# Both MLPs of a decoder step with their first product by Strassen's quadrants, the hidden units through DRAM, and the state-space matrices made beside layer 0's second product

## The chip, the cores and the metric

The kernel runs on one core of a Trainium2 chip. Its time is the device time of one execution in microseconds. Three runs of the kernel before took 2729.11, 2738.31 and 2733.10 us, the median 2733.1. One further execution was profiled: it took 2730.87 us, and 2729.1 us lie between its first and its last instruction (the span). All times of instructions below are from that execution.

## The reference

One inference step through four sublayers: layer 0 has an attention and convolution mixer and an MLP, layer 1 a state-space mixer (S5) and an MLP. A prompt of 1024 tokens and 8 x 4 sample tokens go through the same weights. All is float32. The MLP, with its norms before and after and its residual, is what the change rewrites:

```python
D_MODEL = 1024; D_FF = 4 * D_MODEL
def sq_relu_mlp(xn, w_up, w_down):
    return jnp.square(jax.nn.relu(xn @ w_up)) @ w_down
...
hp = hp + rms_norm(sq_relu_mlp(rms_norm(hp, g_ffn_pre[l]), w_ffn_up[l], w_ffn_down[l]), g_ffn_post[l])
hs = hs + rms_norm(sq_relu_mlp(rms_norm(hs, g_ffn_pre[l]), w_ffn_up[l], w_ffn_down[l]), g_ffn_post[l])
```

The state-space mixer runs a diagonal complex recurrence with 64 groups of 64 states. Its matrices depend on the weights alone (a, b, c and the time step):

```python
dt = jnp.exp(log_dt)[:, None]
mag = jnp.exp(a_re * dt); ang = a_im * dt
ab_re, ab_im = mag * jnp.cos(ang), mag * jnp.sin(ang)
...
bu = einsum('blgc,gpc->blgp', ug, bb)           # real and imaginary part
h = associative_scan over the tokens            # h_t = ab * h_(t-1) + bu_t
y = einsum('blgp,gcp->blgc', h_re, c_re) - einsum('blgp,gcp->blgc', h_im, c_im)
```

## The kernel before

The activations are kept transposed: 8 tiles of 128 features by 1056 tokens, worked on in three chunks of 352 tokens. Every large product is done in split precision: each operand is a high part (`zh`, `whi`, `hh`) and a low part (`zl`, `wlo`, `hl`), and one product of 128 by 128 by 352 is three matmuls (`mm3`, L190): high by high, low by high, high by low. `block` (L197) strings them over the k tiles of one output tile. The high part is a cast on ScalarE (L186, L216), the low part a subtraction on VectorE (L187, L217). SBUF holds 48 slabs of 128 x 1056 float32, handed out and taken back in program order, and some half tiles of 352.

`ffn` (L481) runs one MLP as a list of units. An up unit makes 128 hidden features: 3 chunks of 24 matmuls, each evicted by VectorE (relu times the norm's factor, L502), squared on ScalarE (L503) and split into `hh` and `hl`, which stay in SBUF. After a group of hidden units (2 in layer 0, 4 in layer 1) come down units, which multiply the group by a piece of the second weight matrix and add the result to the eight output tiles `y` (L537). Weights are loaded two units ahead (`wprep`, L179). The last four down units lie inside `posts` (L386), chunk by chunk, each followed by `post` (L303): norm, residual, and the split of the next layer's operands.

What runs beside is a generator: `bg_add` and `pump` (L100, L104) advance it by so many microseconds of its own estimates per unit of the MLP, times a rate. `params5` (L1599) makes the state-space matrices: factors on VectorE, ten doublings of a rotation, then on GpSimd sixteen tables of 128 x 1024, each built from the rotations by complex products (`cmul`, L1590 and on) and written to DRAM (`tabs<-tc`), then b and c, which are turned on TensorE (`cT`, L1766) and combined on GpSimd into eight blocks (`bd`, `ws`, `tmat`). In before it is started ahead of layer 0's MLP with rate 0.7 (`tile_step`, L2103).

A scheduler sets the order of the compute instructions of each engine from its own estimates and the dependencies. Each engine then runs its list strictly in that order. All DMAs of the program go through one queue, SP's (`dma`, L92), and they keep the order in which the program issues them: a transfer whose data isn't ready holds back every transfer behind it.

## Time and profile before

| | |
|---|---|
| runs | 2729.11, 2738.31, 2733.10 us (median 2733.1) |
| profiled execution | 2730.87 us, span 2729.1 us |
| granted TensorE clock, mean | 0.968 |
| TensorE busy | 2562.5 us, 94% of the span |
| VectorE, ScalarE, GpSimd busy | 1573.2, 984.3 and 739.7 us |
| moved by DMA | 276.72 MB, mean 101 GB/s |

The page's busy time is an average over the whole program. By stretch, layer 0's MLP lies from about 760 to 1440 us of the span and layer 1's from about 1990 to the end. A matmul's record is longer than the distance to the next one, since they are pipelined: the price of one in a full stream is the stretch divided by the number of matmuls, or the distance of two starts. On SP a row is one transfer's issue; a transfer that waits appears late, with the reason in the waits.

### The profile page before, as it was taken

Reading aid. Unit: us, or ns where it says so; the run is one execution under the profiler, and the core shown is the slowest. Engines: PE = TensorE matmul, PEld = TensorE weight load, DVE = VectorE, ACT = ScalarE, POOL = GpSimd, SP = SyncE. Lnnn points to the kernel's source line nnn. Section 1 sums busy time; section 2 is a strip of 40 time slices with the busy share of each in tenths; the row PEclk is TensorE's granted clock in tenths of the full one; section 3 lists DMA queues with packets and bytes.
Section 4 is the critical chain, followed back from the end, with each engine's and each line's share of the span. In section 5 each row is a group of like instructions: output and inputs, shape, how many; then the busy total and the mean of one; then the engine's idle time right before and its main releaser. Section 6 shows DMA issues by size and latency. Waiting matters only on the chain. (4 is left out here: it accounts for less than half of the span.)

```text
span 2729.1 us, 41453 instructions
## 1 busy us (share of the span) xinstructions
PE 2562.5 (94%) x15979; PEld 2431.6 (89%) x15979; DVE 1573.2 (58%) x2802; ACT 984.3 (36%) x2032; POOL 739.7 (27%) x1090
## 2 busy tenths in 40 slices
PE   8999889789899999999998888799899999999998
PEld 7999756559799999999998877699799999999997
DVE  6776666753967555655545998941833334333335
ACT  6133355744441212123224566633533112211223
POOL 0110001111607874344303588611600000000004
PEclk9999989999899999999999999899899999999999
DMA  6353689563132223122312533113121111111121
GB/s 188 94 171 113 203 289 325 169 206 94 44 97 60 88 86 92 52 89 83 104 55 66 170 116 131 40 30 118 59 89 55 47 47 47 42 44 40 55 95 64
DMA packets 244828, 276.72 MB, mean 101 GB/s; under 512 B 26452, under 2 KB 179810, under 8 KB 244623
## 3 DMA queue, kind: packets, MB, share of 16 engines
q1 hardware_dynamic: 244299, 273.84, 31.6%
q8 instruction: 126, 2.06, 0.3%
q14 instruction: 71, 0.58, 0.1%
q10 hardware_dynamic: 332, 0.23, 0.0%
HBM read 218.03 MB, written 56.42 MB: 101 GB/s over the span
## 5 line engine op out<-in xcount | busy, mean ns | idle before, releaser
L193 PE MATMUL mm<-hh,whi 128*128 128x352 f32 x1536 | 500.9, 326 | 0.0
L195 PE MATMUL mm<-hh,wlo 128*128 128x352 f32 x1536 | 496.9, 323 | 0.0
L194 PE MATMUL mm<-hl,whi 128*128 128x352 f32 x1536 | 496.7, 323 | 0.0
L193 PE MATMUL mm<-zh,whi 128*128 128x352 f32 x1344 | 448.1, 334 | 0.2 <-ACT zh L216 0.2
L194 PE MATMUL mm<-zl,whi 128*128 128x352 f32 x1344 | 440.5, 328 | 3.9 <-DVE zl L217 3.9
L195 PE MATMUL mm<-zh,wlo 128*128 128x352 f32 x1344 | 438.2, 326 | 0.0
L537 DVE TENSOR_TENSOR y<-y,mm 128x352 f32<-128x352 f32 x456 | 229.9, 518 | 236.6 <-PE mm L195 234.8
L503 ACT ACTIVATE t<-t 128x352 f32<-128x352 f32 x192 | 95.3, 498 | 738.3 <-DVE t L502 738.3
L187 DVE TENSOR_TENSOR wlo<-wraw,whi 128x1024 fp32r<-128x1024 f32 x180 | 229.0, 1275 | 229.6 <-ACT whi L186 225.4
L291 POOL TENSOR_TENSOR ssq<-ssq,sq 128x352 f32<-128x352 f32 x72 | 72.8, 1011 | 955.5 <-issue 672.7
L193 PE MATMUL mm<-gh,whi 128*128 128x352 f32 x960 | 314.5, 328 | 0.0
L194 PE MATMUL mm<-gl,whi 128*128 128x352 f32 x960 | 311.7, 325 | 0.0
L195 PE MATMUL mm<-gh,wlo 128*128 128x352 f32 x960 | 311.5, 324 | 0.0
L193 PEld LDWEIGHTS mm<-hh,whi 128*128 128x128 f32 x1536 | 289.8, 189 | 0.6 <-issue 0.2
L194 PEld LDWEIGHTS mm<-hl,whi 128*128 128x128 f32 x1536 | 289.9, 189 | 0.5 <-issue 0.2
L195 PEld LDWEIGHTS mm<-hh,wlo 128*128 128x128 f32 x1536 | 289.6, 189 | 0.0
L186 ACT CAST whi<-wraw 128x1024 fp32r<-128x1024 f32 x180 | 187.3, 1044 | 245.9 <-DMA wraw<-in_w_ffn_up 77.9
L194 PEld LDWEIGHTS mm<-zl,whi 128*128 128x128 f32 x1344 | 258.0, 192 | 8.1 <-DVE zl L217 4.7
L193 PEld LDWEIGHTS mm<-zh,whi 128*128 128x128 f32 x1344 | 257.3, 192 | 5.9 <-issue 3.3
L195 PEld LDWEIGHTS mm<-zh,wlo 128*128 128x128 f32 x1344 | 257.4, 192 | 0.1
L502 DVE SCALAR_TENSOR_TENSOR t<-mm,r 128x352 f32<-128x352 f32 x192 | 99.9, 524 | 222.3 <-PE mm L195 220.8
L194 PEld LDWEIGHTS mm<-gl,whi 128*128 128x128 f32 x960 | 182.4, 190 | 1.0 <-issue 0.5
(485 smaller groups left out, 4564.9 us busy)
## 6 DMA issues: line engine op xcount, KB each, us to landing
pg<-in_cache_k SPq DMA_DIRECT2D x128, 256.0 KB
pg<-in_cache_v SPq DMA_DIRECT2D x128, 256.0 KB
wraw<-in_w_ffn_up SPq DMA_DIRECT2D x64, 512.0 KB
wraw<-in_w_ffn_down SPq DMA_DIRECT2D x64, 512.0 KB
hres<-res SPq DMA_DIRECT2D x24, 528.0 KB
res<-y SPq DMA_DIRECT2D x24, 528.0 KB
wraw<-in_w_in_even SPq DMA_DIRECT2D x20, 512.0 KB
tabs<-tc SPq DMA_DIRECT2D x16, 512.0 KB
```

The lines of the kernel that those rows point to most:

```text
L186: nc.scalar.copy(hi[:, :n], raw[:, :n])
L187: (eng or nc.vector).tensor_sub(lo[:, :n], raw[:, :n], hi[:, :n])
L193: nc.tensor.matmul(out, wh, xh, start=first, stop=False)
L194: nc.tensor.matmul(out, wh, xl, start=False, stop=False)
L195: nc.tensor.matmul(out, wl, xh, start=False, stop=last)
L291: (nc.vector if k in YV else nc.gpsimd).tensor_add(s, s, q)
L502: nc.vector.scalar_tensor_tensor(t1, pt, 0.0, r[:, chunk(c)], op0=ALU.max, op1=ALU.mult)
L503: nc.scalar.activation(t1, t1, AF.Square)
L537: nc.vector.tensor_add(yc, yc, pt)
```

## The change

The first product of each MLP is restated. The first four units (512 hidden features) are done as before. For the other 28, two units at a time, weights and activations are cut in quadrants (two halves of the 1024 features; two halves of the 256 hidden features; two halves of 528 tokens), and seven products of the quadrants' sums take the place of eight. Each product has 4 k tiles and 528 tokens in two pieces of 264. `sums` makes the sums of the activations as a background generator, started where the previous layer's `post` ends; `quads` makes and splits those of the weights, pair by pair, from slabs whose load is issued at the start of the pair before. The seven results are combined on the way out of PSUM in two slabs `hu` and `hv`, which get relu, factor and square over all 1056 tokens and are stored to DRAM. All 32 hidden units are loaded from DRAM again (`hr`) and split for the second product, now in eight groups of four, each step of which is 6 tiles of 12 matmuls of 352 columns. The state-space matrices are no longer started ahead of layer 0's MLP but between its two products (`beside`), with rate 1.4.

```diff
--- before
+++ after
 CH = 352
 NCH = T // CH
+T2 = T // 2
 DFF = 4096
...
             for k in range(KT):
                 self.dma(nxt[2][k], y[k])
+            if nxt[5]:
+                self.T = [[None] * 4 for _ in range(4)]
+                self.bg_add(self.sums(list(y), g2, l2, self.T), TR)
...
+    def sums(self, y, gk, l, T_):
+        nc = self.nc
+        a, b = slice(0, T2), slice(T2, T)
+        for k in range(4):
+            z1, z2 = y[k], y[k + 4]
+            y[k] = y[k + 4] = None
+            for z, k_ in ((z1, k), (z2, k + 4)):
+                nc.scalar.activation(z, z, AF.Copy, scale=self.g(gk, l, k_))
+                yield 1.1
+            nc.vector.tensor_sub(z2[:, b], z2[:, b], z1[:, b])
+            nc.vector.tensor_sub(z1[:, b], z1[:, b], z1[:, a])
+            yield 1.2
+            T_[0][k] = self.S("t1", F32R)
+            self.split(T_[0][k][:, a], T_[0][k][:, b], z1[:, b])
+            nc.vector.tensor_add(z1[:, a], z2[:, b], z1[:, a])
+            yield 1.2
+            nc.vector.tensor_sub(z2[:, a], z2[:, a], z1[:, a])
+            T_[1][k] = self.S("t2", F32R)
+            self.split(T_[1][k][:, a], T_[1][k][:, b], z1[:, a])
+            yield 1.2
+            T_[3][k] = self.S("t4", F32R)
+            self.split(T_[3][k][:, a], T_[3][k][:, b], z2[:, a])
+            T_[2][k] = z2
+            z1 = None
+            yield 1.2
+    def quads(self, R):
+        nc = self.nc
+        (a11, a21), (a12, a22) = ([r[:, :1024].rearrange("p (k j m) -> p j k m", k=4, j=2)[:, j] for j in range(2)] for r in R)
+        def part(x):
+            o = self.S("op", F32R)
+            v = [o[:, 512 * i:512 * i + 512].rearrange("p (k m) -> p k m", k=4) for i in range(2)]
+            self.split(v[0], v[1], x)
+            return v
+        yield part(a11)
+        s1 = self.S("s1")[:, :512].rearrange("p (k m) -> p k m", k=4)
+        nc.vector.tensor_add(s1, a21, a22)
+        nc.vector.tensor_sub(a21, a11, a21)
+        nc.vector.tensor_sub(a11, s1, a11)
+        yield part(a11)
+        yield part(a12)
+        nc.vector.tensor_sub(a12, a12, a11)
+        yield part(a21)
+        yield part(s1)
+        s1 = None
+        yield part(a12)
+        yield part(a22)
 
...
+    def ffn_q(self, l, X, r, res, nxt, early=None, beside=None):
+        nc = self.nc
+        w, self.pre = self.pre, {}
+        hd = self.dram.tile([32, P, T], F32, name=self.nm("hid"))
+        up_w = self.a["w_ffn_up"][l]
+        raws = {}
+        slot = [None, 3]
+        def raw(u):
+            if u < 32:
+                raws[u] = [self.S("wq") for _ in range(2)]
+                for i in range(2):
+                    self.dma(raws[u][i][:, :1024].rearrange("p (k m) -> p k m", k=4),
+                             up_w[512 * i:512 * i + 512, u * P:(u + 2) * P].rearrange("(k p) m -> p k m", p=P))
+        def up(u, c):
+            pt = self.block(w[u], slice(0, P), X, c)
+            t1 = self.H("t")
+            nc.vector.scalar_tensor_tensor(t1, pt, 0.0, r[:, chunk(c)], op0=ALU.max, op1=ALU.mult)
+            if slot[1] == 3:
+                slot[:] = self.S("hp"), 0
+            h = slot[0][:, chunk(slot[1])]
+            slot[1] += 1
+            nc.scalar.activation(h, t1, AF.Square)
+            self.dma(hd[u][:, chunk(c)], h)
+            self.pump(3.7)
+        for u in range(NB):
+            if u not in w:
+                w[u] = self.ffn_prep(l, ("u", u))
+        ops = []
+        for c in range(NCH):
+            self.chunk_ready(c)
+            if c == NCH - 1:
+                raw(NB)
+                steps = self.quads(raws[NB])
+            for u in range(NB):
+                up(u, c)
+                if c == NCH - 1:
+                    del w[u]
+                    if u:
+                        ops.append(next(steps))
+        slot[0] = None
+        self.drain()
+        B = T2
+        for k in range(4):
+            z = self.T[2][k][:, B:]
+            self.split(X[k][0][:, B:], X[k][1][:, B:], z)
+            self.T[2][k] = z = None
+        both = lambda t: [(z[:, :B], z[:, B:]) for z in t]
+        lo, hi = slice(0, B), slice(B, T)
+        rhs = [[(h[:, lo], l_[:, lo]) for h, l_ in X[:4]], both(self.T[1]), [(h[:, lo], l_[:, lo]) for h, l_ in X[4:]],
+               [(h[:, hi], l_[:, hi]) for h, l_ in X[:4]], both(self.T[0]), [(h[:, hi], l_[:, hi]) for h, l_ in X[4:]],
+               both(self.T[3])]
+        self.T = None
+        hid, wd = {}, {}
+        seq = [("d", 4 * f, 4, j) for f in range(8) for j in range(4)]
+        def prep(i):
+            if i < len(seq) and i not in wd:
+                wd[i] = self.ffn_prep(l, seq[i])
+        def hload(u):
+            if u < 32 and u not in hid:
+                z = self.S("hr")
+                self.dma(z, hd[u])
+                hid[u] = self.S("hh", F32R), self.S("hl", F32R)
+                self.split(*hid[u], z)
+        def ahead():
+            prep(0)
+            yield
+            for u in range(4):
+                if u == 2:
+                    prep(1)
+                hload(u)
+                yield
+        first, more = True, None
+        for u in range(NB, 32, 2):
+            hu, hv = self.S("hu"), self.S("hv")
+            nxt_ops = []
+            if u == 30:
+                more = ahead()
+            else:
+                raw(u + 2)
+            nsteps = None
+            for p in range(7):
+                while len(ops) <= p:
+                    ops.append(next(steps))
+                wh, wl = ops[p]
+                for x in range(2):
+                    xs = slice(264 * x, 264 * x + 264)
+                    pt = self.PS("mq")[:, :264]
+                    for k in range(4):
+                        xh, xl = rhs[p][k]
+                        self.mm3(pt, (wh[:, k], wl[:, k]), (xh[:, xs], xl[:, xs]), k == 0, k == 3)
+                    c0, c1 = slice(264 * x, 264 * x + 264), slice(B + 264 * x, B + 264 * x + 264)
+                    if p == 0:
+                        nc.scalar.copy(hu[:, c0], pt)
+                    elif p == 1:
+                        nc.vector.tensor_add(hu[:, c1], hu[:, c0], pt)
+                    elif p == 2:
+                        nc.vector.tensor_add(hu[:, c0], hu[:, c0], pt)
+                    elif p == 3:
+                        nc.vector.tensor_add(hv[:, c0], hu[:, c1], pt)
+                    elif p == 4:
+                        nc.vector.tensor_add(hu[:, c1], hu[:, c1], pt)
+                        nc.vector.tensor_add(hv[:, c1], hv[:, c0], pt)
+                    elif p == 5:
+                        nc.vector.tensor_add(hu[:, c1], hu[:, c1], pt)
+                    else:
+                        nc.vector.tensor_add(hv[:, c0], hv[:, c0], pt)
+                wh = wl = None
+                ops[p] = None
+                if p == 5:
+                    nc.vector.scalar_tensor_tensor(hu, hu, 0.0, r, op0=ALU.max, op1=ALU.mult)
+                    nc.scalar.activation(hu, hu, AF.Square)
+                    self.dma(hd[u], hu)
+                if more is not None:
+                    next(more, None)
+                elif p >= 0:
+                    if nsteps is None:
+                        nsteps = self.quads(raws[u + 2])
+                        raws.pop(u, None)
+                    nxt_ops.append(next(nsteps))
+            nc.vector.scalar_tensor_tensor(hv, hv, 0.0, r, op0=ALU.max, op1=ALU.mult)
+            nc.scalar.activation(hv, hv, AF.Square)
+            self.dma(hd[u + 1], hv)
+            ops, steps = nxt_ops, nsteps
+        X.clear()
+        rhs = xh = xl = hu = hv = nsteps = nxt_ops = pt = ops = steps = more = None
+        raws.clear()
+        for u in range(4):
+            hload(u)
+        if beside is not None:
+            beside()
+        y = [None] * KT
+        last = len(seq) - 4
+        for i, (_, f, g, j) in enumerate(seq[:last]):
+            prep(i + 2)
+            hload(f + 4 + j)
+            hs = [hid[f + i_] for i_ in range(4)]
+            for m in range(2):
+                k = 2 * j + m
+                if f == 0:
+                    y[k] = self.S("y")
+                for c in range(NCH):
+                    pt = self.block(wd[i], slice(m * P, (m + 1) * P), hs, c)
+                    yc = y[k][:, chunk(c)]
+                    if f == 0:
+                        nc.scalar.copy(yc, pt)
+                    else:
+                        nc.vector.tensor_add(yc, yc, pt)
+                    self.pump(1.84)
+            del wd[i]
+            if j == 3:
+                for i_ in range(4):
+                    del hid[f + i_]
+        for j in range(4):
+            prep(last + j)
+        self.drain()
+        hs = [hid[28 + i_] for i_ in range(4)]
...
     with s.psum():
         s.consts()
         X, r, res = s.mixer0()[:3]
-        s.bg_add(s.params5(), RP)
         nxt = s.new(X, "g_mix_pre", 1)
-        s.ffn(0, X, r, res, nxt, 2, s.mixer1_early)
+        s.ffn_q(0, X, r, res, nxt, s.mixer1_early, lambda: s.bg_add(s.params5(), RP))
         X, r, res = s.mixer1(*nxt[:3])[:3]
-        s.ffn(1, X, r, res, None, 4)
-
-
-RP = 0.7
+        s.ffn_q(1, X, r, res, None)
+RP = 1.4
```

(`new` gets a flag that asks for the sums; both callers ahead of an MLP set it.)

The scheduler's order changes with it. First, SP's queue in layer 0 near the end of the sixteen tables. `tabs` are the tables, `wraw` a weight load, `hr` a hidden unit, `b` and `cn` the state-space inputs. Before:

```order
L94 DMA wraw_1598_11206<-in_w_ffn_up 128x8x128
L94 DMA wraw_1613_11326<-in_w_ffn_up 128x8x128
L94 DMA tabs_7769<-tc_1597_11197 128x1024
L94 DMA wraw_1629_11456<-in_w_ffn_down 128x2x512
L94 DMA tabs_7769<-tc_1618_11349 128x1024
L94 DMA b_1638_11525<-in_ssm_b_re 64x32x16 x2
L94 DMA b_1638_11525<-in_ssm_b_im 64x32x16 x2
L94 DMA wraw_1643_11562<-in_w_ffn_down 128x2x512
L94 DMA wraw_1654_11666<-in_w_ffn_up 128x8x128
```

After, in the second product:

```order
L96 DMA wraw_1837_13511<-in_w_ffn_down 128x4x256
L96 DMA hr_1840_13517<-hid_1208_7736 128x1056
L96 DMA tabs_11610<-tc_1836_13496 128x1024
L96 DMA wraw_1850_13647<-in_w_ffn_down 128x4x256
L96 DMA hr_1853_13653<-hid_1208_7736 128x1056
L96 DMA tabs_11610<-tc_1846_13578 128x1024
L96 DMA tabs_11610<-tc_1857_13674 128x1024
L96 DMA b_1862_13758<-in_ssm_b_re 64x32x16 x2
L96 DMA b_1862_13758<-in_ssm_b_im 64x32x16 x2
L96 DMA wraw_1866_13779<-in_w_ffn_down 128x4x256
L96 DMA hr_1869_13785<-hid_1208_7736 128x1056
L96 DMA cn_1878_13855<-in_ssm_c_re 128x8x64 x2
```

Between two tables there were one or two weight loads; now two tables often stand with none between them, and a hidden unit goes with each weight load. From the first to the sixteenth table the new queue holds nine weight loads (before, nineteen).

Second, VectorE between the first four units on the last chunk and what follows them in layer 0. Before (`t<-mm` is an eviction, `hl` a low half):

```order
L502 SCALAR_TENSOR_TENSOR t_1273_8248<-mm_1272_8223,r_1123_7176 128x352
L217 TENSOR_TENSOR hl_1271_8222<-t_1273_8248,hh_1270_8221 128x352
L1629 COPY hs_1212_7771<-hT_1274_8253 64x256 x2
L1641 MEMSET nat_1282_8335 64x128
L502 SCALAR_TENSOR_TENSOR t_1276_8283<-mm_1275_8258,r_1123_7176 128x352
L217 TENSOR_TENSOR hl_1271_8222<-t_1276_8283,hh_1270_8221 128x352
L502 SCALAR_TENSOR_TENSOR t_1279_8318<-mm_1278_8293,r_1123_7176 128x352
L1629 COPY hs_1212_7771<-hT_1280_8323 64x256 x2
```

After (`y` are the tokens' sums, `t1`, `t2`, `t4` and `op` operands of the seven products, `wq` weight quadrants):

```order
L219 TENSOR_TENSOR t2_1260_8191<-y_1054_6784,t2_1260_8191 128x528
L459 TENSOR_TENSOR y_1062_6851<-y_1108_7107,y_1062_6851 128x528
L485 TENSOR_TENSOR s1_1262_8199<-wq_1247_8080,wq_1248_8081 128x512
L219 TENSOR_TENSOR t4_1261_8194<-y_1104_7064,t4_1261_8194 128x528
L461 TENSOR_TENSOR y_1108_7107<-y_1108_7107,y_1062_6851 128x528
L486 TENSOR_TENSOR wq_1247_8080<-wq_1247_8080 128x4x128
L487 TENSOR_TENSOR wq_1247_8080<-s1_1262_8199,wq_1247_8080 128x4x128
L219 TENSOR_TENSOR op_1263_8203<-wq_1247_8080,op_1263_8203 128x512
L219 TENSOR_TENSOR t1_1266_8237<-y_1062_6851,t1_1266_8237 128x528
L219 TENSOR_TENSOR t2_1267_8242<-y_1062_6851,t2_1267_8242 128x528
L219 TENSOR_TENSOR op_1268_8245<-wq_1248_8081,op_1268_8245 128x512
```

`op_1263` and `t2_1267` are operands of the second of the seven products; from the eviction of the first unit to `t2_1267` VectorE's list now holds three evictions and 36 sums and low halves.

Third, TensorE at the first transpose of C, in layer 0's MLP. Before:

```order
L193 MATMUL mm_1668_11741<-hh_1632_11462,whi_1631_11459 128x352
L194 MATMUL mm_1668_11741<-hl_1633_11463,whi_1631_11459 128x352
L195 MATMUL mm_1668_11741<-hh_1632_11462,wlo_1630_11457 128x352
L1766 MATMUL cT_1669_11749<-ident_69,cn_1662_11698 128x128 x4
L193 MATMUL mm_1670_11754<-hh_1589_11098,whi_1631_11459 128x352
```

After, in the second product's 17th step (`hh_1814` is a hidden unit read from DRAM, `whi_1839` the weights of the 16th):

```order
L195 MATMUL mm_1880_13872<-hh_1814_13237,whi_1839_13514 128x352
L196 MATMUL mm_1880_13872<-hl_1815_13238,whi_1839_13514 128x352
L197 MATMUL mm_1880_13872<-hh_1814_13237,wlo_1838_13512 128x352
L2005 MATMUL cT_1881_13886<-ident_69,cn_1878_13855 128x128 x4
L2005 MATMUL cT_1882_13893<-ident_69,cn_1878_13855 128x128 x4
L195 MATMUL mm_1889_13910<-hh_1827_13379,whi_1852_13650 128x352
```

The transposes moved from a place among the mixed units to the head of the 17th of 28 steps of the second product, with the list behind them unchanged in kind.

## Rows read from the trace of the kernel before

**Rows 1.** The page's first part: busy time, share of the span and instructions of each engine.
```profile
PE 2562.5 (94%) x15979; PEld 2431.6 (89%) x15979; DVE 1573.2 (58%) x2802; ACT 984.3 (36%) x2032; POOL 739.7 (27%) x1090
```

**Rows 2.** Busy time by stretch: length, then each engine's busy us (instructions).
```profile
core 0: us, PE busy (x) PEld busy (x) DVE busy (x) ACT busy (x) POOL busy (x), PEclk, DMA share, GB/s
800.00:1400.00 600.00, 600.00 (x3791) 599.36 (x3790) 349.03 (x765) 142.68 (x232) 299.62 (x614) 1.00 0.27 80
2100.00:2600.00 500.00, 500.00 (x3108) 500.00 (x3107) 185.49 (x305) 102.97 (x171) 0.00 (x0) 1.00 0.15 46
850.00:1057.00 207.00, 207.00 (x1290) 207.00 (x1289) 114.20 (x202) 44.80 (x73) 169.98 (x404) 1.00 0.28 87
1057.00:1355.00 298.00, 298.00 (x1914) 297.36 (x1914) 164.87 (x314) 74.15 (x119) 114.26 (x172) 1.00 0.28 80
690.00:710.00 20.00, 11.65 (x56) 10.87 (x55) 15.37 (x24) 9.64 (x21) 13.79 (x13) 0.74 0.06 18
```

**Rows 3.** Timeline of TensorE near 359 us: start, duration, engine, line, operation, shapes.
```profile
358.78 0.28 PE L1085 MATMUL sp<-kh__431_3270,qp 128*128 128x256 f32 x1
358.90 0.28 PE L1086 MATMUL sp<-kl__432_3271,qp 128*128 128x256 f32 x1
359.02 0.23 PE L1088 MATMUL sp<-keep,keep 128*128 128x128 bf16 x1
```

**Rows 4.** Groups of instructions: busy us, mean ns of one, idle time before them.
```profile
L187 DVE TENSOR_TENSOR wlo<-wraw,whi 128x1024 fp32r<-128x1024 f32 x180 | 229.0, 1275 | 229.6 <-ACT whi L186 225.4 <-DMA pg<-in_cache_k 3.2 <-issue 0.4
L738 DVE SCALAR_TENSOR_TENSOR acc<-proj,keep,acc 128x1024 f32<-128x1024 f32 x120 | 156.5, 1304 | 3.0
L1921 DVE TENSOR_TENSOR w<-x,tb 128x256 f32<-128x256 f32 x32 | 13.0, 408 | 2.6 <-PE x L1914 2.6
...
L186 ACT CAST whi<-wraw 128x1024 fp32r<-128x1024 f32 x180 | 187.3, 1044 | 245.9 <-DMA wraw<-in_w_ffn_up 77.9 <-DMA wraw<-in_w_ffn_down 55.6 <-PE mm L195 51.0
```

**Rows 5.** Timeline of VectorE, layer 0's first four units on the last chunk.
```profile
763.04 0.53 DVE L502 SCALAR_TENSOR_TENSOR t<-mm,r 128x352 f32<-128x352 f32 x1 [1.60 <-PE mm L195]
...
774.61 0.53 DVE L502 SCALAR_TENSOR_TENSOR t<-mm,r 128x352 f32<-128x352 f32 x1 [1.72 <-PE mm L195]
```

**Rows 6.** Timeline of SP's queue and of ScalarE: a weight load and its reader.
```profile
2107.65 0.37 SPq L94 DMA_DIRECT2D wraw<-in_w_ffn_up  x1
...
2111.79 1.05 ACT L186 CAST whi<-wraw 128x1024 fp32r<-128x1024 f32 x1 [0.80 <-DMA wraw<-in_w_ffn_up]
```

**Rows 7.** Timeline of SP's queue: tables (first, three in a row, last) and b.
```profile
859.68 0.34 SPq L94 DMA_DIRECT2D tabs<-tc  x1
...
1004.36 0.34 SPq L94 DMA_DIRECT2D tabs<-tc  x1
...
1015.14 0.34 SPq L94 DMA_DIRECT2D tabs<-tc  x1
...
1025.61 0.34 SPq L94 DMA_DIRECT2D tabs<-tc  x1
...
1056.92 0.34 SPq L94 DMA_DIRECT2D tabs<-tc  x1
1057.31 2.40 SPq L94 DMA_DIRECT2D b<-in_ssm_b_re  x2
```

**Rows 8.** Waits of SP's queue, 840 to 1060 us: total us, times, longest.
```profile
SPq L94 <- POOL tt L1593: 79.7, 6, 18.3
```

**Rows 9.** Timeline of GpSimd: two products of the tables, then the first block of states.
```profile
1012.82 1.47 POOL L1596 TENSOR_TENSOR tt<-tc,keep 128x256 f32<-128x256 f32 x1
...
1024.15 0.61 POOL L1596 TENSOR_TENSOR tt<-tc,keep 128x256 f32<-128x256 f32 x1
...
1111.15 2.78 POOL L1772 TENSOR_SCALAR nq<-cq 128x1024 f32<-128x1024 f32 x1 [11.72 <-DVE cq L1770]
...
1120.21 1.70 POOL L1809 TENSOR_TENSOR bd<-ws 64x256 f32<-64x256 f32 x2
```

**Rows 10.** GpSimd's copies ahead of the tables, 847 to 1058 us.
```profile
L1733 POOL COPY tc<-tb 128x32 f32<-128x32 f32 x30 | 8.1, 298 | 21.4 <-PE mm L194 15.0 <-PE mm L195 6.4
```

More of the change, by code (lines that the diff above doesn't have):

```diff
@@ L30 @@
 XA = ()
+TR = 1.0
 HP, YV, PE, EP = (0, 2), (7,), 14.0, ((1, 1), (2, 1))
@@ L315, in post @@
             if nxt is not None:
-                X, rn, rs, g2, l2 = nxt
+                X, rn, rs, g2, l2 = nxt[:5]
                 self.split(X[k][0][:, chunk(c)], X[k][1][:, chunk(c)], yc, self.g(g2, l2, k))
@@ L432, in chunk_ready, with new @@
             self.factor(1)
-    def new(self, X, g, l):
-        return X, self.S("r"), self.dram.tile([KT, P, T], F32, name=self.nm("res")), g, l
+    def new(self, X, g, l, sums=False):
+        return X, self.S("r"), self.dram.tile([KT, P, T], F32, name=self.nm("res")), g, l, sums
+    def sums(self, y, gk, l, T_):
[44 more added lines that the diff above has]
+        yield part(a22)
     def store(self, y, c):
@@ L550, in product @@
                 pt = self.block(w[last + k // 2], slice((k % 2) * P, (k % 2 + 1) * P), hs, c)
+                yc = y[k][:, chunk(c)]
+                nc.vector.tensor_add(yc, yc, pt)
+                self.ysum(y[k], c, k, s)
+                yield 1.85
+        self.posts(y, product, 14.8, "g_ffn_post", l, res, nxt, early)
+    def ffn_q(self, l, X, r, res, nxt, early=None, beside=None):
[140 more added lines that the diff above has]
+                    pt = self.block(wd[i], slice(m * P, (m + 1) * P), hs, c)
+                    yc = y[k][:, chunk(c)]
+                    if f == 0:
+                        nc.scalar.copy(yc, pt)
+                    else:
+                        nc.vector.tensor_add(yc, yc, pt)
+                    self.pump(1.84)
[7 more added lines that the diff above has]
+        hs = [hid[28 + i_] for i_ in range(4)]
+        if nxt is not None:
+            nxt[0].extend((self.S("zh", F32R), self.S("zl", F32R)) for _ in range(KT))
+        def product(c, s):
+            for k in range(KT):
+                pt = self.block(wd[last + k // 2], slice((k % 2) * P, (k % 2 + 1) * P), hs, c)
@@ L1465, in mixer0 @@
         X = Z + [(self.S("zh", F32R), self.S("zl", F32R)) for _ in range(4)]
-        nxt = self.new(X, "g_ffn_pre", 0)
+        nxt = self.new(X, "g_ffn_pre", 0, True)
         def product(c, s):
@@ L2093, in mixer1 @@
         self.states_out()
-        nxt = self.new(G, "g_ffn_pre", 1)
+        nxt = self.new(G, "g_ffn_pre", 1, True)
         self.gemm_post(wo, G, "g_mix_post", 1, res, nxt, lambda: self.ffn_early(1, 4))
```

## The prediction, made before the changed kernel was run

> **What bounds the kernel now.** I read the page's first part, then the busy time by stretch, then what waits inside the stretches that the change touches. TensorE is busy 2562.5 us of the 2729.1 us span [rows 1]. By stretch it is busier still where the change is made: 600.00 of 600.00 us between 800 and 1400 us (layer 0's MLP) and 500.00 of 500.00 between 2100 and 2600 (layer 1's MLP), at a granted clock of 1.00 [rows 2]. Nothing waits there, so each MLP costs what its matmuls cost, end to end, and the other engines have slack: in the first of these stretches VectorE is busy 349 us, ScalarE 143, GpSimd 300 of 600. The change takes matmul time out, and everything it adds is free only as long as TensorE finds its operands ready. The question is therefore where the new order makes TensorE wait.
>
> **Term 1, fewer and narrower matmuls.** One MLP has 28 units of 72 matmuls of 352 columns that become 14 pairs of 168 matmuls of 264: 2016 become 2352. In layer 1's stretch 3108 matmuls (nearly all of 352 columns) fill 500.00 us, 160.9 ns each [rows 2]. No row shows 264 columns; the nearest are the two starts of 256-column matmuls: 358.78, 358.90, 359.02, so 120 ns [rows 3]. A line through both widths, (160.9 - 120)/96 = 0.426 ns a column, gives 123.4 ns at 264. So 324.4 us become 2352 x 123.4 = 290.2: -34 us a layer, -68 for both. Bounds: 112 ns if most of the cost beside the columns vanishes (-61 a layer), 126 ns from the rounding of the starts to 0.01 us (-28). I take the line, which lies 8 columns from a measured width. The Trainium skill's page "TensorE: Matmul & The Clock Gate", section "Back-to-back issue gap", gives N/2.4 + 2.5 ns for an isolated warm matmul, that is 112.5 ns at 264; by it the layer saves 60 us. The same rule makes 149 ns at 352 columns where this trace has 160.9, so I don't go by it in the sum, and it is a rival below.
>
> **Term 2, the loop of a pair in the new first product.** A pair takes TensorE 168 x 123.4 ns = 20.7 us. VectorE has in that time 14 additions of 264 columns out of PSUM (a 256-column one takes 408 ns, so about 0.42), 7 low halves and 4 sums of 512 columns (1275 ns for 1024 and 0.53 for 352, so about 0.71) and 2 products of 1056 columns (1304 for 1024, so about 1.31): 5.9 + 7.8 + 2.6 = 16.3 us [rows 4, 5]. That fits. ScalarE's part is smaller. The hidden units' way through DRAM, 17.3 MB a layer each way, falls on DMA engines with a share of 0.27 and 0.15 [rows 2] and costs nothing by itself. But the weights of the next pair are issued on SP behind the hidden store of the pair before, which waits for the last product (1.3) and the square (about 1.1 by the 1044 ns cast [rows 4]); then the transfer: a weight slab issued at 2107.65 was read at 2111.79, 4.1 us [rows 6]; then a cast. VectorE's order puts the first split of these weights early in the pair and 13 to 15 us of its work behind it. Around that loop: 13 to 15 + 1.1 + about 1 of SP + 4.1 + 0.6 = 20 to 22 us, against 20.7. Loss per pair 0 to 1.4 us, over 14 pairs 0 to 20 us a layer. I take 4 a layer, near the lower end since half of the loop's range is under 20.7: +8 for both.
>
> **Term 3, the sums ahead of the second product.** The quarters of the activations are combined on VectorE while the first four units run on the last chunk. Before, VectorE's row between two such units is nearly empty; now 36 additions, subtractions and low halves of 528 or 512 columns stand between the eviction of unit 0 of chunk 2 and the last operand that product 2 needs (the second order above). At about 0.70 us each plus three evictions of 0.53 that is 26.8 us. VectorE starts on it at 763.6, after the eviction at 763.04, and ends near 790.4 [rows 5]. TensorE is through with the four units at 774.6 (the fourth eviction's start) and with product 1, 2 halves of 12 matmuls or 3 us, at 777.6. It waits 12.8 us there, about 2.5 more at product 4, whose weights are split behind it, and 1 for a lower clock after the gap (the one stretch with long gaps in these rows, 690 to 710, ran at 0.74 [rows 2]). +16 a layer, +32 for both; bounds 8 (ScalarE's and VectorE's work at 0.5 us a piece, as the narrow rows have it) and 20.
>
> **Term 4, the state-space matrices beside the second product alone.** This decides the sign. Before, the generator runs beside all of layer 0's MLP and its sixteen tables leave on SP's queue between 859.68 and 1056.92, one every 13.1 us on the mean, 10.8 and 10.5 us at the closest [rows 7]. GpSimd makes them and is busy 170 of the 207 us [rows 2], so 10.8 us of GpSimd a table. SP's queue stands waiting for GpSimd most of that time: 79.7 us at one line alone [rows 8]. TensorE doesn't notice, since in before's order one or two weight loads stand between two tables (the first order above) and one unit of work covers 11.6 us.
>
> Now the same tables go with a queue that also has to feed the second product, in a phase of 28 steps of 72 x 160.9 ns = 11.6 us (325 us with what follows). VectorE's order puts the end of the rotation factors, which every table needs, behind the eviction of tile 42: 81 us after the start D of the second product. The first table leaves at about D+86, the sixteenth at D+86 + 15 x 10.8 = D+248. Between the first and the sixteenth stand nine weight loads, nine steps or 104 us of TensorE's work, for 162 us of tables. Behind the sixteenth stand step 17's weights and the hidden unit 19 that step 16's tiles read. Step 16 would start at D + 16 x 11.6 = D+185; its hidden unit is issued some 6 us behind the table (four loads of b ahead of it, of which the first two took 2.40 us of the queue in before [rows 7]), lands 4.1 us later and is split in 2.3: D+260, 75 us late. The transposes of C, which the queue brings next, stand in TensorE's order at the head of the same step (third order above), and the first table of states at its seventh tile: two tiles for the imaginary part (6 us), 1.5 for the copy and 10.8 us of GpSimd (1111.15 to 1121.9 in before [rows 9]) give D+278 for what stands at D+199: +79. After that a block of states takes GpSimd 114 us over 8 in all (114.26 busy between 1057 and 1355 [rows 2]), 14 us each, and TensorE's own order has 14 to 16 us for one, so nothing further is lost or won back. I take +80. Bounds: 10.5 us a table gives +74, before's mean of 13.1 gives 15 x 13.1 = 197 and +114; if VectorE's and GpSimd's chain gets ahead of where I put it by a step or two, +50.
>
> A rule of the Trainium skill bears on the price of a table. The 256-column product took GpSimd 1.47 us at 1012.82 and 0.61 at 1024.15 [rows 9], both alike in shape. The "GPSIMD Engine Reference", section "Specifications", says that GpSimd's SBUF interfaces are shared with VectorE; by it a TensorE that waits would also quieten VectorE and a table would go toward its undisturbed 10.5 us: 5 us less in the sum.
>
> **Sum.** Against the profiled execution's 2730.9 us: -68 + 8 + 32 + 80 = +52, 2783 us; the three runs have their median 2.2 us above that execution, so 2785.
>
> **Rivals.**
> (a) The tables hide. If the two steps' lead of the weight loads and the tiles' freedom cover the queue, term 4 is nothing and the sum is -68 + 40: 2730.9 - 28 + 2.2 = 2705, faster. For it: before made the same tables with TensorE at 100%. Against: there the queue had a weight load for each table, here nine for sixteen, and a lead of two steps is 23 us against 60. It decides if a table costs less than 104/15 + 23/15 = 8.5 us, which no interval of rows 7 shows.
> (b) The matmul's fixed part vanishes at 264 columns, the rule above: 112.5 ns a matmul, -26 more a layer, 2733, no change. TensorE's 18 us a pair would lie under the loop of term 2, so I give it little.
> (c) The loop of a pair ends last: 22 to 23 us for 20.7 in 28 pairs, +56 in place of +8: 2833, slower. For it: the store, the load, the split and the next additions hang on one another; against: VectorE has 4 us of slack a pair.
> (d) GpSimd's tables wait for slabs that the late steps free, so both sides wait for each other: before has 21.4 us of such waits at GpSimd's copies ahead of a table [rows 10]; then 13.1 us a table, +114: 2819.
>
> **Chances.** My forecast 0.62, (a) 0.12, (b) 0.06, (c) 0.09, (d) 0.11. A change under 0.3% (8 us) is about what a measurement of this kernel can't tell from none. Faster comes from (a) and a part of (b): 0.13; the same from (b) and the low edges of the sum: 0.07; slower from the rest: 0.80. The likeliest case's own range is 2752 to 2822: term 1 +12/-54, term 2 -8/+32, term 3 -16/+8, term 4 -30/+34, which don't all fall one way. For 8 in 10 I reach down toward (b) and up to (c): 2738 to 2832.
>
> **What would show it.** TensorE's busy share in layer 1's first product near 100% with starts 123 ns apart, right for term 1; an idle stretch of 10 to 16 us ahead of product 2, ended by VectorE, in both layers, right for term 3. In layer 0's second product TensorE idle some 80 us in pieces, mostly ended by a DMA of weights or hidden units or by work on C, and SP's queue waiting for GpSimd between tables 10 to 11 us apart, right for term 4. The forecast is wrong if TensorE stays above 97% busy through layer 0's second product (then (a)), or if the idle time of the first product is spread over all pairs at more than 2 us each (then (c)).

## The result, and the profile after

The changed kernel takes 2809.9 us in the median (2803.4 to 2813.3), the kernel before 2732.9: a ratio of 1.0277, with a 95% interval of 1.0251 to 1.0304. That is 77 us slower. The forecast was 2785 us, in a range of 2738 to 2832, and "slower" with a chance of 0.80. The profiled execution of after took 2807.9 us.

Where the 77 us lie is read from four places in both traces: the start of the matmul right behind the norm's column sum in the first chunk of layer 0's MLP, of layer 1's mixer and of layer 1's MLP, and the end of the span.

| stretch | from, before | from, after | us before | us after | difference |
|---|---|---|---|---|---|
| up to layer 0's MLP | 0 | 0 | 715.31 | 714.22 | -1.1 |
| layer 0's MLP | 715.31 | 714.22 | 792.84 | 893.42 | +100.6 |
| layer 1's mixer | 1508.15 | 1607.64 | 436.20 | 436.76 | +0.6 |
| layer 1's MLP, to the end | 1944.35 | 2044.40 | 784.7 | 761.7 | -23.0 |

The same rewriting gains 23 us in layer 1 and loses 101 in layer 0. What layer 0 has besides is the state-space matrices beside its second product: 123.6 us by this difference, against the 80 of the forecast. Read inside the second product alone it is 118 us (the working stands with term 4 below); of the other 5, layer 1 gains 2 more than layer 0 ahead of the products of quadrants and 3 more behind the second product.

The page's first part of after, to compare with [rows 1]:

```profile
span 2806.1 us, 43683 instructions
PE 2513.6 (90%) x16651; PEld 2374.3 (85%) x16651; DVE 1762.7 (63%) x3102; ACT 1049.0 (37%) x2036; POOL 739.9 (26%) x1090
```

TensorE is busy 49 us less and the span is 77 us longer.

Busy time by stretch of after (first products at 820 to 1060 and 2130 to 2370, layer 0's second product from 1079 on), to compare with [rows 2]:

```profile
core 0: us, PE busy (x) PEld busy (x) DVE busy (x) ACT busy (x) POOL busy (x), PEclk, DMA share, GB/s
820.00:1060.00 240.00, 240.00 (x1974) 240.00 (x1973) 171.62 (x320) 77.31 (x128) 0.00 (x0) 1.00 0.30 102
1079.00:1160.00 81.00, 81.00 (x503) 79.88 (x502) 54.73 (x219) 24.66 (x39) 11.28 (x25) 1.00 0.30 101
1160.00:1360.00 200.00, 122.47 (x667) 119.50 (x665) 63.37 (x119) 19.12 (x18) 175.10 (x422) 0.80 0.30 97
1360.00:1400.00 40.00, 33.08 (x200) 32.75 (x200) 19.35 (x36) 8.49 (x9) 28.01 (x38) 0.88 0.38 120
1400.00:1590.00 190.00, 177.63 (x1116) 175.76 (x1115) 106.10 (x186) 54.85 (x75) 106.42 (x151) 0.96 0.40 137
2130.00:2370.00 240.00, 239.85 (x1968) 239.64 (x1967) 170.06 (x316) 75.96 (x126) 0.00 (x0) 1.00 0.29 99
```

Both first products run with TensorE at 240.00 and 239.85 of 240 us and at full clock: 240/1974 = 121.6 ns for a matmul of 264 columns. The trouble begins at 1160: of 200 us TensorE works 122.47, at a granted clock of 0.80, while GpSimd is busy for 175.

What TensorE waited for in layer 0's second product of after (us in total, times, longest):

```profile
PE mm L195 <- ACT whi L188: 47.8, 6, 11.8
PE cT L2005 <- DMA cn<-in_ssm_c_re: 28.3, 1, 28.3
PE sT L2066 <- POOL bd L2047: 11.7, 4, 3.6
PE mm L197 <- DVE wlo L189: 4.9, 2, 4.8
```

Weights cast from a late load, the transposes of C, and the blocks: 92.7 us without the column sum (`cs`), which waits much the same in before. The hidden units' loads by themselves cost nothing: layer 1's second product has the same loads without the matrices, and TensorE is busy 345.00 of 345 us there (2407 to 2752). The queue that brings the weights, SP's, in the same stretch of after, to compare with [rows 7] (start, duration; `x2` is a row of two issues):

```profile
1177.61 0.33 SPq L96 DMA_DIRECT2D tabs<-tc  x1
1178.00 0.43 SPq L96 DMA_DIRECT2D wraw<-in_w_ffn_down  x1
1178.47 0.89 SPq L96 DMA_DIRECT2D hr<-hid  x1
1189.27 11.15 SPq L96 DMA_DIRECT2D tabs<-tc  x2
...
1339.43 10.41 SPq L96 DMA_DIRECT2D tabs<-tc  x2
1349.94 2.29 SPq L96 DMA_DIRECT2D b<-in_ssm_b_re  x2
...
1355.15 1.48 SPq L96 DMA_DIRECT2D wraw<-in_w_ffn_down  x1
1356.74 0.44 SPq L96 DMA_DIRECT2D hr<-hid  x1
1357.23 1.05 SPq L96 DMA_DIRECT2D cn<-in_ssm_c_re  x2
```

The first table leaves at 1177.61, that is 98 us after the start of the second product at 1079.3, the sixteenth at about 1349.5: 172 us for fifteen tables, 11.5 each. A weight load and a hidden unit go out at once after a table and then the queue stands. What SP's queue waited for between 1165 and 1360 us, against [rows 8]:

```profile
SPq L96 <- POOL tt L1832: 109.9, 6, 56.7
SPq L96 <- POOL tc L1972: 61.1, 6, 10.3
SPq L96 <- POOL tc L1836: 40.8, 4, 10.9
```

212 us of waiting for GpSimd in a stretch of 195 (the first of these waits began ahead of it): the queue did next to nothing else. And TensorE at the first transpose of C:

```profile
1363.49 1.94 PE L2005 MATMUL cT<-ident,cn 128*128 128x128 f32 x8 [28.32 <-DMA cn<-in_ssm_c_re]
```

It begins 284 us after the start of the second product, for a place in the list that is worth 185 us of matmuls.

The passage from the first four units to the products of quadrants in layer 0 of after, TensorE's timeline:

```profile
777.67 0.59 PE L195 MATMUL mq<-zh,op 128*128 128x264 f32 x1 [9.30 <-ACT op L218]
...
783.49 0.59 PE L197 MATMUL mq<-zh,op 128*128 128x264 f32 x1 [4.58 <-DVE op L219]
...
789.16 0.59 PE L195 MATMUL mq<-t,op 128*128 128x264 f32 x1 [0.90 <-ACT op L218]
...
799.84 0.59 PE L195 MATMUL mq<-zh,op 128*128 128x264 f32 x1 [2.87 <-ACT op L218]
```

Four waits, 17.7 us; the profile names the operand cast from a weight quadrant. The first two, 13.9 us, stand at the first of the seven products (24 matmuls lie between 777.67 and the third wait), 0.9 us at the second, 2.9 at the fourth. The load of the first pair's weights leaves SP's queue only when TensorE has run out of the four units (768.4):

```profile
771.00 1.02 SPq L96 DMA_DIRECT2D wq<-in_w_ffn_up  x2
```

Behind the first waits TensorE runs slowly (a row of the busy time by stretch, granted clock 0.50):

```profile
777.67:792.85 15.18, 9.70 (x41) 9.08 (x41) 14.46 (x25) 6.24 (x13) 0.00 (x0) 0.50 0.31 100
```

Layer 1 has the same four, 17.8 us.

### The profile page after: what moved, and what is told of

Read it like the earlier page. It is cut to its first block, busy times and chain, and to the rows that moved or that the text cites. A ratio compares the mean times of both kernels' runs of the same rounds, so it can differ in the third digit from the quotient of the medians.

```text
span 2806.1 us, 43683 instructions
## 1 busy us (share of the span) xinstructions
PE 2513.6 (90%) x16651; PEld 2374.3 (85%) x16651; DVE 1762.7 (63%) x3102; ACT 1049.0 (37%) x2036; POOL 739.9 (26%) x1090
## 5 line engine op out<-in xcount | busy, mean ns | idle before, releaser
L195 PE MATMUL mm<-zh,whi 128*128 128x352 f32 x672 | 227.7, 341 | 0.2 <-ACT zh L218 0.2
L196 PE MATMUL mm<-zl,whi 128*128 128x352 f32 x672 | 221.0, 329 | 2.7 <-DVE zl L219 2.7
L197 PE MATMUL mm<-zh,wlo 128*128 128x352 f32 x672 | 219.3, 327 | 0.0
L218 ACT CAST op<-wq 128x512 fp32r<-128x512 f32 x168 | 95.9, 618 | 292.2 <-DMA wq<-in_w_ffn_up 118.8
L195 PE MATMUL mq<-t,op 128*128 128x264 f32 x672 | 192.3, 287 | 1.8 <-ACT op L218 1.8
L196 PE MATMUL mq<-t,op 128*128 128x264 f32 x672 | 192.5, 287 | 0.0
L197 PE MATMUL mq<-t,op 128*128 128x264 f32 x672 | 191.6, 287 | 0.2 <-DVE op L219 0.2
L195 PE MATMUL mm<-xh,whi 128*128 128x352 f32 x480 | 159.0, 333 | 5.2 <-DVE xr L281 5.2
L977 DVE SCALAR_TENSOR_TENSOR acc<-proj,keep,acc 128x1024 f32<-128x1024 f32 x120 | 156.4, 1303 | 3.0
L196 PE MATMUL mm<-xl,whi 128*128 128x352 f32 x480 | 156.3, 327 | 0.0
L197 PE MATMUL mm<-xh,wlo 128*128 128x352 f32 x480 | 156.0, 326 | 0.0
L195 PE MATMUL mq<-gh,op 128*128 128x264 f32 x448 | 129.2, 289 | 12.3 <-ACT op L218 12.3
```

The costliest lines, as they stand in the source:

```text
L195: nc.tensor.matmul(out, wh, xh, start=first, stop=False)
L196: nc.tensor.matmul(out, wh, xl, start=False, stop=False)
L197: nc.tensor.matmul(out, wl, xh, start=False, stop=last)
L218: nc.scalar.copy(hi, x)
L977: nc.vector.scalar_tensor_tensor(acc[:, :NP], u[:, i:i + NP], w[:, k, i:i + 1], acc[:, :NP], op0=ALU.mult, op1=ALU.add)
```

## Experiments

**Layer 1 alone (e1).** Layer 0 keeps the MLP of before with the matrices beside all of it:

```diff
-        nxt = self.new(X, "g_ffn_pre", 0, True)
+        nxt = self.new(X, "g_ffn_pre", 0)
...
+        s.bg_add(s.params5(), RP)
         nxt = s.new(X, "g_mix_pre", 1)
-        s.ffn_q(0, X, r, res, nxt, s.mixer1_early, lambda: s.bg_add(s.params5(), RP))
+        s.ffn(0, X, r, res, nxt, 2, s.mixer1_early)
...
-RP = 1.4
+RP = 0.7
```

> The quadrants in layer 1 alone; layer 0's MLP and the matrices' place as in the kernel before. The comparison of the two traces puts layer 1's MLP 23 us shorter and the whole loss into layer 0. If the two layers don't touch each other: 2733 - 23 = 2710 us (2703 to 2717). If layer 1's gain needs something that layer 0's change does to it (slabs, order, clock), it comes out within 8 us of 2733.

Measured: 2710.1 us (2706.1 to 2712.2), 0.9911 of before (0.9885 to 0.9936). The two layers don't touch each other, and the whole loss is layer 0's. This version beats both kernels.

**The tables on a queue of their own (e2).**

```diff
-            self.dma(self.tabs[m], tc_[:, :1024])
+            self.tc.keep_in_program_order(nc.gpsimd.dma_start(self.tabs[m], tc_[:, :1024]))
```

> The changed kernel, with the sixteen tables written to DRAM on GpSimd's own DMA queue, so that no weight load or hidden unit stands behind one. Theory 'queue' (the loads behind the tables cost the time): the 53 us of waits for weights and about 20 us of low clock after them go, 2735 us. Theory 'chain' (98 us to the first table, 16 tables at 11.5, 27 to the first block, 8 blocks at 14: some 410 us of dependent work against 325 us of cover, wherever it is met): TensorE runs freely to the transposes of C in the 17th step and waits there instead, some 85 us in one piece in place of 28; only a part of the low clock is won: 2790 to 2805 us.

Measured: 2773.7 us (2770.8 to 2782.7), 36 less than after and outside both ranges. TensorE's waits in layer 0's second product:

```profile
PE sT L2066 <- POOL bd L2047: 52.1, 8, 14.4
PE cT L2005 <- DMA cn<-in_ssm_c_im: 5.9, 1, 5.9
```

The waits for casts of weights are gone, as "queue" has it; in their place TensorE waits 52 us for the blocks (`bd`). C's transposes wait only 6 us, since `cn` is no longer behind the tables either; I had put the wait one place too early. GpSimd's list after the ninth table and at the last:

```profile
1299.37 0.59 POOL L1979 DMA_DIRECT2D tabs<-tc  x1 [0.30 <-POOL tc L1836]
...
1312.50 1.49 POOL L2047 TENSOR_TENSOR bd<-ws 64x256 f32<-64x256 f32 x2
...
1477.64 0.59 POOL L1979 DMA_DIRECT2D tabs<-tc  x1 [0.30 <-POOL tc L1836]
```

So the blocks don't wait until the tables are through: with the tables off SP's queue the scheduler mixes the last seven of them with the blocks. What holds TensorE is GpSimd's amount of work (busy 174.5 of 190 us from 1300 to 1490), and "chain" is right in that and not in the order that it assumed. The 36 us are worth the queue and this new order together, out of some 120; most of the rest is met a few tiles further on.

**Half the tables on VectorE (e3).** `en` is VectorE for odd tables, which have a scratch tile of their own:

```diff
+            en = nc.vector if m % 2 else nc.gpsimd
...
-                nc.gpsimd.tensor_copy(tv[i][:, :, :16], tbv[i][:, xs, :])
+                en.tensor_copy(tv[i][:, :, :16], tbv[i][:, xs, :])
```

> The changed kernel, with every second table made on VectorE instead of GpSimd; queue and order of the loads unchanged. Theory 'chain': sixteen tables take some 100 us instead of 172, the end comes 70 us and some clock earlier: 2725 to 2755 us. Theory 'queue': nine loads' worth of work (104 us) then covers the tables, the waits for weights go as well: 2735 to 2755 us. If neither the tables' rate nor their queue matters (clock, hidden units' traffic): 2800 to 2815.

Measured: 2772.6 us (2763.8 to 2775.1), 37 less than after, 18 us above the range of both theories. TensorE's waits:

```profile
PE cT L2008 <- DMA cn<-in_ssm_c_re: 22.3, 1, 22.3
PE mm L195 <- ACT whi L188: 19.5, 4, 8.7
PE sT L2069 <- POOL bd L2050: 12.8, 4, 3.6
PE mm L197 <- DVE wlo L189: 5.9, 2, 4.8
```

53 us of waits for weights became 25, and the rest nearly stayed. VectorE's list holds its tables between evictions and splits of weights, which waited 11.4 us for TensorE and 23.6 for ScalarE's casts between 1160 and 1330, so the fifteen intervals of the tables took 135 us (1178.3 to 1313.6) in place of 172, and not 100. That the tables' rate counts is shown; my price for it was too good.

**Both (e5).**

> Both edits together. Theory 'chain': as with half the tables on VectorE alone, within 15 us below it, 2715 to 2750. Theory 'queue': as with the own queue alone, within 10 us of it, since the tables' rate then matters to nobody.

Measured: 2744.8 us (2743.6 to 2751.9), 65 less than after and 29 less than the own queue alone. So the rate still matters when nothing stands behind a table in the queue: theory "queue" alone is refuted. It is also 28 less than half the tables alone, where "chain" allowed 15: the queue costs something beside the chain, and the two gains, 36 and 37, nearly add up. TensorE's waits, of which the first is still the blocks:

```profile
PE sT L2069 <- POOL bd L2050: 21.5, 4, 12.0
PE mm L196 <- DVE hl L219: 12.1, 3, 8.8
```

**An earlier start, alone (e11) and with both (e10).** The generator's first estimate, which holds back the whole work, is cut, and the tables' estimates are stretched so that C's transposes and the blocks keep their places in TensorE's list:

```diff
-        yield 30.0
+        yield 2.0
...
-                yield 0.6 + 0.03 * n
+                yield 1.0375 + 0.03 * n
```

> The changed kernel (2810 us) with only that start, 21 us earlier; queue and tables as they were, fewer loads behind the first tables. Theory 'chain': 20 to 28 us less, 2782 to 2790. Theory 'queue': the same sixteen tables stand ahead of the same last loads and now begin earlier as well, so it expects the same 2782 to 2790; if the lateness doesn't hang on the chain's start at all (each load's own way), 2803 to 2815.

> Tables half on VectorE and written on GpSimd's queue (2745 us), and the matrices' work started 11 tiles (21 us) earlier, with the places of C's transposes and of the blocks in TensorE's list unchanged. Theory 'chain' (the end of the dependent work sets how late TensorE is): 21 us less lateness and the low clock behind it, 2712 to 2726 us. Rival 'rate' (what is left is lost in the blocks, which GpSimd makes more slowly than TensorE's list comes to them): 2735 to 2748.

Measured: 2798.5 us (2792.7 to 2802.4) for the start alone, 11 less than after; 2739.7 (2734.9 to 2743.4) with both, 5 less than without the start. Both miss. The intervals of the ratios to before overlap in both pairs (1.0225 to 1.0265 against after's 1.0251 to 1.0304, and 1.0005 to 1.0030 against 1.0027 to 1.0058), so that the medians alone don't settle these gains; the traces show the second product 12.1 us shorter in the first pair (478.3 for 490.4) and 3.4 in the second (423.4 for 426.8). TensorE's waits of the one with the start alone, in layer 0's second product:

```profile
PE cT L2005 <- DMA cn<-in_ssm_c_re: 28.6, 1, 28.6
PE mm L195 <- ACT whi L188: 19.3, 5, 6.3
PE mm L196 <- DVE hl L219: 14.8, 4, 9.8
```

The waits for weights fell from 53 to about 20 us, so the start was worth some 30 us where I had looked. But 15 came back in the first seven steps: `hl` are low halves of the hidden units, and in the longest of these waits (9.8 us, 78 us after the product's start) VectorE's list has the rotation's small operations ahead of them. A chain that starts earlier displaced work that the second product starts with. Its end came earlier by what the product gained: the first table leaves 82 us after the product's start in place of 98, the sixteenth 258 in place of 270, and C's transposes begin at 272 in place of 284.

**Spread (e12).** With the early start and both edits of the tables, the rotation's doublings are estimated at twice their former value (so they lie twice as far apart), and C's transposes and the blocks come four tiles later:

```diff
                 z = z2
-                yield 1.0
+                yield 2.0
...
-                yield 0.6 + 0.03 * n
+                yield 1.06 + 0.03 * n
```

> As with the early start, half the tables on VectorE and their own queue (2740 us), with the rotation's doublings spread over twice as many tiles (VectorE's splits of the first hidden units no longer queue behind them) and C's transposes and the blocks four tiles later in TensorE's list. Theory 'chain, and VectorE's list at the start': 19 us of waits in the first steps fall to about 8, 12 us ahead of the blocks to about 4, with some low clock: 2714 to 2726 us. If the blocks' own rate on GpSimd holds what is left: 2732 to 2742.

Measured: 2739.5 us (2733.8 to 2747.1), no better than e10. TensorE's waits:

```profile
PE sT L2069 <- POOL bd L2050: 11.4, 4, 3.6
PE mm L196 <- DVE hl L219: 10.1, 4, 4.9
```

The waits for `hl` fell by 5 us only (14.8 with e10), those ahead of the blocks hardly (11.8), though the blocks stand four tiles later. That fits the rival of the expectation: these last waits are small ones, block by block, at GpSimd's own pace.

**Layer 1 without the activations' sums (e6).**

```diff
-        rhs = [[(h[:, lo], l_[:, lo]) for h, l_ in X[:4]], both(self.T[1]), ...
-               [(h[:, hi], l_[:, hi]) for h, l_ in X[:4]], both(self.T[0]), ...
-               both(self.T[3])]
+        rhs = [[(h[:, lo], l_[:, lo]) for h, l_ in X[:4]], [(h[:, hi], l_[:, hi]) for h, l_ in X[4:]], ...
+               [(h[:, hi], l_[:, hi]) for h, l_ in X[:4]], [(h[:, hi], l_[:, hi]) for h, l_ in X[:4]], ...
+               [(h[:, lo], l_[:, lo]) for h, l_ in X[:4]]]
```

> The quadrants in layer 1 alone (2710 us), with the activations' sums left out: four of the seven products read quarters of the activations themselves in place of sums of quarters, so the output isn't the reference's; matmuls, weights' sums and order of the products stay. Theory 'sums' (TensorE's 17 us of waits ahead of products 2 to 4 are VectorE's, whose list holds the sums ahead of the weights' sums): the waits go, 2692 to 2698 us. Rival 'weights' (the wait is for the first pair's weights, loaded on the last chunk; the profile names an operand cast from them): the waits stay, 2705 to 2712.

Measured: 2699.3 us (2697.4 to 2701.9), 11 less than e1 (9 by the ratios to before, 0.9879 and 0.9911), between the two. TensorE in layer 1 with the sums (e1):

```profile
2007.14 0.59 PE L195 MATMUL mq<-gh,op 128*128 128x264 f32 x1 [7.70 <-ACT op L218]
...
2012.82 0.59 PE L197 MATMUL mq<-gh,op 128*128 128x264 f32 x1 [4.43 <-DVE op L219]
...
2018.49 0.39 PE L195 MATMUL mq<-t,op 128*128 128x264 f32 x1 [1.11 <-ACT op L218]
...
2027.79 0.59 PE L195 MATMUL mq<-gh,op 128*128 128x264 f32 x1 [2.94 <-ACT op L218]
```

and without (e6):

```profile
2003.21 0.59 PE L195 MATMUL mq<-gh,op 128*128 128x264 f32 x1 [3.82 <-ACT op L218]
...
2015.98 0.39 PE L195 MATMUL mq<-gh,op 128*128 128x264 f32 x1 [2.21 <-ACT op L218]
...
2022.20 0.39 PE L197 MATMUL mq<-gh,op 128*128 128x264 f32 x1 [0.15 <-DVE op L219]
```

Of 16 us of waits 10 go with the activations' sums; 6 stay, for operands cast and split from the weights.

**Weights first (e13), and layer 1 alone again (e1b).** In layer 1, the only MLP of the new kind here, the first pair's weights are loaded and summed from the second chunk on:

```diff
-            if c == NCH - 1:
+            if c == 1:
                 raw(NB)
...
-                if c == NCH - 1:
-                    del w[u]
-                    if u:
-                        ops.append(next(steps))
+                if c >= 1 and u:
+                    ops.append(next(steps))
+                if c == NCH - 1:
+                    del w[u]
```

> The quadrants in layer 1 alone, with the first pair's weights loaded and their sums and splits made from the second chunk on, ahead of most of the activations' sums. Without the activations' sums 6 us of waits stayed, with them 16. Theory 'both on VectorE's list': 4 to 7 us less than with the quadrants in layer 1 alone, 2702 to 2707 when that runs at 2710. If the activations' sums alone set it: within 2 us of it.

> The quadrants in layer 1 alone again, on the same chip as the one with the weights first: 2706 to 2714 us.

Measured on one chip: 2708.8 us (2705.6 to 2713.1, ratio to before 0.9912, 0.9896 to 0.9927) against 2712.9 (2709.1 to 2717.5; 0.9924, 0.9910 to 0.9938). 4 us less in the medians, but the intervals of the ratios overlap, so the gain is not settled. The waits for operands of the products sum to 14.6 us in its trace and to 16.4 in its pair's: they moved more than they shrank. At the first product 12.1 became 2.9, but 6.1 stand at the second, where the pair has 1.1, and 5.6 further on. So the weights' place and the activations' sums are not two prices that add up: what waits less for the one waits for the other. The quadrants in layer 1 alone, in either form, are the fastest version here that computes the whole step, 20 to 24 us under before.

## Why the prediction was right, and where it was off

The range held and the sign was right; the forecast of 2785 was 25 us short. That it was no more is in part luck: term 4 came out 44 us too small, beyond its own bounds, and terms 1 and 2 were together 17 us too dear, which covered part of it.

**Term 1** (-34 a layer) measured -38: 264 columns cost 121.6 ns in a full stream, not the 123.4 of the line through 352 and 256. The two-decimal starts of [rows 3] left that open. The trace has 9 ns more than the 112.5 of rival (b), which is out. The Trainium skill's page "TensorE: Matmul & The Clock Gate" (section "Back-to-back issue gap") gives N/2.4 + 2.5 ns for an isolated warm matmul, an estimate of 112.5 ns for this width; this stream, at 121.6, doesn't agree with it.

**Term 2** (+4 a layer) is nothing: TensorE worked 240.00 of 240 us in a stretch of layer 0's pairs. The loop that I put at 20 to 22 us closes in less than the pair's 168 x 121.6 ns = 20.4. Rival (c) is out.

**Term 3** (+16 a layer) came out right on balance and wrong in its working. Layer 1 gained 23.0 us where the matmuls gave 38.4, so 15.4 were lost. The passage itself lost more: 17.8 us of waits in layer 1, and some 7 us in matmuls that ran slowly behind them (from 777.67 to 792.85 in layer 0 the granted clock was 0.50, the lower of the clock's two levels), where the forecast had 1 us for the clock. That is 25 us, over the bound of 20. Some 10 us were won back elsewhere in layer 1's MLP, 5.6 of them ahead of the passage: its first four units take 35.9 us on the first two chunks and took 41.5 in before, with shorter waits at the column sums and a granted clock of 1.00 for 0.89. That the balance comes to the forecast's 16 is luck. The place was wrong, too: 12.8 us were forecast ahead of the second product, for the activations' sums, and 0.9 are there, while some 14 stand at the first product, for its weights. The sums have a share in them (without them 10 of 16 us go, e6), as they stand in the same list as the weights' low halves.

**Term 4** (+80) measured +123.6 by difference and 118 inside the second product, both over its upper bound of 114, and is the step that failed in size. Its mechanism stands: SP's queue waits for GpSimd's tables, nine loads go out between first and sixteenth, TensorE waits for weights, then for C, then for blocks. Two sizes were too small. The first table left 98 us after the start, not 86: GpSimd's first tables wait for the rotation on VectorE up to 1171. A table took 11.5 us, not 10.8, or 10 us over fifteen; rival (d), at 13.1, went too far, and nothing came of the 10.5 for a quieter VectorE, which was busy for only 63 of 200 us there (1160 to 1360). Together the sixteenth table came at 270 us instead of 248, and C's transposes at 284 in place of the forecast's 260: +99 in place of +75. The other mistake is "nothing further is lost or won back": some 20 us more were, 11.7 of them as waits for blocks. The others are time in which TensorE was busy but slow, and I hadn't priced the clock in this term at all. In the whole of the second product some 26 us are of this kind: from its start at 1079.3 to its first column sum at 1569.7 it takes 490.4 us, against 345.2 for the same matmuls in layer 1 (2407.0 to 2752.2); 26.9 are TensorE's own work on the matrices (in before, layer 0's MLP takes 714.7 us from the column sum of the third chunk at 757.1 to that of the norm behind it at 1471.8, layer 1's 687.8 from 1985.8 to 2673.6, both with TensorE busy throughout), 92.7 are waits, and 26 are left. Part of that is seen directly, in the section on the hardware; that all of it is the clock is argued from the granted 0.80, 0.88 and 0.96 of the stretches above and not tested by itself.

The forecast's rival (a), that the tables hide, is refuted by the trace, and its reasoning too: with no table ahead of any load (e2) TensorE still loses some 87 us against two layers at -23 each. The cause of the loss is that the matrices' own work, most of it on GpSimd (98 us to the first table, 172 for the tables, then the inputs and eight blocks), is longer than the product it was put beside, and the queue adds to it: an own queue gives back 36 us, half the tables on VectorE 37, both 65. Some 50 us remained in the best of these (e10, e12), in waits of up to 10 us and behind them low clock; which share is VectorE's crowded list and which is the blocks' rate stays open.

## What to carry to other kernels

Before background work is moved beside a shorter stretch, add up its own work, engine by engine and with the wait of each handover, and compare it with the cover: the busy time of the stretch before (170 of 207 us on GpSimd) already showed that little room was left. A queue that keeps program order makes such a chain everybody's: count what stands behind each transfer that waits. And a change to two like stages is worth running on one of them alone.

## What the runs showed of the hardware

After a wait TensorE restarts slowly. After the longest wait for weights in after (start, duration; the distance of starts is the price of a matmul):

```profile
1206.43 0.66 PE L195 MATMUL mm<-hh,whi 128*128 128x352 f32 x1 [11.76 <-ACT whi L188]
...
1207.19 0.49 PE L195 MATMUL mm<-hh,whi 128*128 128x352 f32 x1
1207.48 0.49 PE L196 MATMUL mm<-hl,whi 128*128 128x352 f32 x1
...
1209.83 0.32 PE L195 MATMUL mm<-hh,whi 128*128 128x352 f32 x1
1209.99 0.33 PE L196 MATMUL mm<-hl,whi 128*128 128x352 f32 x1
```

0.29 us lie between starts right after a gap of 11.8 us, and 0.16 three microseconds later. The granted clock was 0.52 from 1206.43 to 1209.50, the lower of the clock's two levels (1.2 and 2.4 GHz), and 1.00 from 1209.83 to 1213.50. So the waits of this stretch cost more than their sum. And a matmul of 264 columns in a full stream took 121.6 ns where one of 352 took 160.9 [rows 2]: 0.461 and 0.457 ns a column. A quarter fewer columns took a quarter less time, which the two 256-column starts had not shown so plainly.
